# The opening of a hybrid attention block in another order

## The chip, the cores and the metric

The kernel runs on one core of a Trainium2 chip. The metric is the device time of one execution in microseconds (us), lower is better. The core has five engines with a queue of instructions each: PE (matrix multiply; PEld is its loading of weights), DVE (vector), ACT (activations and copies), POOL (general) and SP, which here only issues DMAs. An engine takes its instructions in the order in which the program writes them, and waits where an operand or a buffer is not ready.

## The reference

One layer of a streaming encoder on x of 1024 tokens by 1024 channels, in float32. Only the first part matters here, the two parallel head groups.

```python
h = rmsnorm(x, g_mix_pre[l])
proj = h @ w_in[l]                       # fq, fk, fv, f_logit, cq, ck, cv
f_logit = f_logit + b_fgt[l]
...
def forgetting_attention(q, k, v, f_logit):
    logf = jax.nn.log_sigmoid(f_logit.astype(jnp.float32))
    c = jnp.cumsum(logf, axis=1).transpose(0, 2, 1)
    # logit[t, s] = q_t.k_s / sqrt(Dh) + c[t] - c[s], for s <= t, 8 heads of 64
...
# chunked attention: 8 heads, own chunk of 64 and 8 chunks before, bias by clipped relative position
y = concat(rmsnorm(y_fox), rmsnorm(y_chk))
x = x + rmsnorm(y @ w_out[l], g_mix_post[l])
# then cross-attention into 256 memory tokens, and a squared-ReLU MLP with 4096 hidden channels
```

## The kernel before

Every product is made of three matmuls on high and low halves (`mm3`, lines 172 to 176): ACT copies an operand to its high half, another engine subtracts to get the low half. PE therefore needs both halves of both operands.

**The opening** (lines 1293 to 1480) is written out by hand. x comes in transposed (`load_xt`, tiles `xf`, two token halves of 512) for the products and by rows (`load_row`, `square`) for the norm. `wv_split` makes the halves of the value weights, `plain_split` those of x times the gain `gp`. `value_part` makes the values of a token half and a head group in four PSUM banks (`value_banks`), twelve matmuls for each bank group and channel block `kc`, eight blocks in all. Since the rows' norms come later, `root` turns the squares into factors `rall`, and `values_out` applies them when it empties the banks; for group 0 it also puts the eight forget-gate logits of each token into `fcol`. For q and k, x itself has to be normed: `root` also makes four diagonal pieces, `spread` multiplies them by ones on PE and copies the result to `rt`, `norm` multiplies x by it and `norm_split` makes new halves in the place of the old ones. The order of products is group 0 half 0, group 1 half 0, group 0 half 1, group 1 half 1.

`forget_gates` (lines 377 to 403) transposes `fcol` to eight rows of 1024 tokens, adds the bias `bfgt`, makes the log-sigmoid in steps on DVE and ACT, and scans along the row for `c`. Its last step stores the rows in `cd` (line 401). `bias_rows` loads the relative bias, lays it out and stores it in `rd` (line 229). Both stores are issued by SP where they are written, at the end of the opening.

**The attention phase** is planned at build time. `Flow` keeps a clock of its own: `put` enters a call for an engine (V is DVE, S is ACT, G is POOL, D is SP's DMAs) with the time from which it may run and its assumed cost, `upto` writes the calls in the order that these give, and `run` writes PE's steps from several streams: values, transposes of probabilities, scores, and the fillers, which are the projections of q, k and v (`project_steps`, `filler_steps`). `Tokens` count free buffers, among them six of the shared pool `u4`, and the two PSUM banks `mm` of the projections. `Stock.pump` loads and splits weight blocks in the order q0, k0, q1, k1, q2, ...; the opening itself loads the first three and splits two (`split_now`), and the planner's first step loads the next ones. `Biases.pump` reads `cd` for the biases of the forgetting heads once `seen["gates"]` has passed. `Outputs.pump` starts the first output products when fourteen `u4` buffers are free. The projection of q0 and k0 is made for token half 0 and then for half 1; half 1 of q takes a bank that half 0 of q has left (lines 691 to 698).

Of the kernel before, what the change touches and what calls it, by code (L numbers as in the profile page):

```python
# [135 lines left out]
def build(ctx, tc, nc, out, t):  # L136
# [58 lines left out]
    bfgt = const.tile([8, 1], F32, name="bfgt")  # L195
# [23 lines left out]
    def bias_rows(part):  # L219
# [9 lines left out]
        nc.sync.dma_start(rd, rrow)  # L229
# [147 lines left out]
    def forget_gates():  # L377

        z, e, l, u = [p1.tile([8, S], F32, tag="klo", bufs=4, name=f"f{n}") for n in "zelu"]
        parts = []  # L380
        for g in range(2):
            tr = mm_tile([8, 4, P], f"ftr{g}", "mm")
            for j in range(4):
                nc.tensor.transpose(tr[:, j, :], fcol[:, g * 4 + j, :], ident)
            parts.append(("V", 0.75, lambda g=g, tr=tr: nc.vector.tensor_scalar(
                z[:, g * HT:(g + 1) * HT], tr.rearrange("p a b -> p (a b)"), bfgt, None, op0=ALU.add)))

        parts += [
            ("V", 0.7, lambda: nc.vector.tensor_scalar(l, z, -1.0, None, op0=ALU.mult)),
            ("V", 1.2, lambda: nc.vector.tensor_tensor(l, l, z, op=ALU.min)),  # L390
            ("S", 1.1, lambda: nc.scalar.activation(e, l, AF.Exp)),
            ("V", 0.7, lambda: nc.vector.tensor_scalar(u, e, 1.0, None, op0=ALU.add)),
            ("S", 2.4, lambda: nc.scalar.activation(l, u, AF.Ln)),
            ("V", 1.3, lambda: nc.vector.scalar_tensor_tensor(e, u, 1.0, e, op0=ALU.subtract, op1=ALU.subtract)),
            ("S", 2.4, lambda: nc.scalar.activation(u, l, AF.Exp, scale=-1.0)),
            ("V", 1.2, lambda: nc.vector.tensor_tensor(e, e, u, op=ALU.mult)),
            ("V", 1.2, lambda: nc.vector.tensor_sub(e, e, l)),
            ("V", 1.3, lambda: nc.vector.scalar_tensor_tensor(e, z, 0.0, e, op0=ALU.min, op1=ALU.add)),
            ("V", 0.9, lambda: nc.vector.memset(u, 0.0)),
            ("V", 2.3, lambda: nc.vector.tensor_tensor_scan(l, e, u, 0.0, op0=ALU.add, op1=ALU.add)),  # L400
            ("D", 0.55, lambda: nc.sync.dma_start(cd, l))]

        return [call for _, _, call in parts]
# [54 lines left out]
    def score_steps():  # L458
# [5 lines left out]
        for n, a in heads:  # L464
            kind, pr = ORDER[n]
            h = pr * 2 + a
            for g in groups(n):
                probs[n, a, g] = {}
                for q in (1, 0) if kind == "f" else (0, 1):
# [9 lines left out]
                    for j, (o, w) in enumerate(pieces):  # L479
# [21 lines left out]
                        if not last:  # L501
                            flow.put("V", flow.end, 0.1 + w / 1000, reduce, free["s"].give)
                        else:
# [6 lines left out]
                            rest = [("S", 0.25 + nk / 1090, exp), ("V", 0.17, inv), ("G", 0.25 + nk / 1150, mul)]  # L510
# [10 lines left out]
                            go = lambda at, w=w, reduce=reduce, after=after: flow.put("V", at, 0.1 + w / 1000, reduce, after)  # L521
# [329 lines left out]
    class Outputs:  # L851
# [5 lines left out]
        def pump(self):  # L857
            while self.left:
                th, g = self.left[0]
                if not (there(("od", g)) and ((th, g) == (0, 0) or there("keys")) and free["u4"].ready(14 if (th, g) == (0, 0) else 9)):  # L860
                    break
# [431 lines left out]
    with tc.manual_schedule():  # L1293
# [34 lines left out]
        for i in range(2):  # L1328
            list(load_wv(1, i))
        vs = [[u4(f"vs{g}_{i}", (P, 2, 4, P)) for i in range(4)] for g in range(2)]  # L1330
        for kp in range(2):
            list(load_xt(1, kp))
        for b in range(3):
            load_row(b)
        for kp in range(2, 4):
            list(load_xt(1, kp))

        def wv_split(g, i, eng, cut=False):
# [6 lines left out]
            for c in (slice(0, 1), slice(1, n)) if cut else (slice(0, n),):  # L1345
                nc.scalar.activation(w[0][:, c, :], raw[:, c, :], AF.Copy)
                eng.tensor_sub(w[1][:, c, :], raw[:, c, :], f(w[0][:, c, :]))
            return [(w[0][:, j, :], w[1][:, j, :]) for j in range(n)]
# [17 lines left out]
        def root(th):  # L1366
# [4 lines left out]
            for b in range(4):  # L1371
                nc.gpsimd.tensor_scalar(d[:, b, :], ident, r[:, b:b + 1], 1.0, op0=ALU.mult, op1=ALU.mult)
# [42 lines left out]
        w0 = wv_split(0, 0, nc.vector, True)  # L1415
        for kc in range(3):
# [23 lines left out]
        for kc in range(2):  # L1440
            plain_split(1, kc)
        values_out(0, 0, V)
        for kc in range(2, 4):
            plain_split(1, kc)
        spread(0, d, "s")
        for kc in range(4, 8):
            plain_split(1, kc)
        for kc in range(4):
            norm(0, kc)
# [701 lines left out]
```

## Time and profile before

| | |
|---|---|
| time, median of 3 runs | 1519.47 us (1517.37 to 1520.83) |
| the profiled execution | 1516.47 us, span 1514.7 us |
| mean granted PE clock | 0.993 |
| PE busy | 1468.5 us (97%) |
| DVE busy | 929.5 us (61%) |
| ACT busy | 795.5 us (53%) |
| POOL busy | 390.7 us (26%) |

The profile is of one execution. The span runs from its first instruction to its last; the time holds a little more. A view of one engine's instructions gives start, duration, engine, line, operation, output and input, and in brackets the idle time just before with what ended it. A matmul's end is modelled.

### The profile page before, as it was taken

What the parts mean: (1) busy time and instruction counts of PE and PEld (TensorE: products, weight loads), DVE (VectorE), ACT (ScalarE), POOL (GpSimd) and SP (SyncE); (2) the same over time, 40 slices, a digit from 0 to 9 for tenths busy, and PEclk for the clock granted to TensorE, in tenths of its full rate; (3) what the DMA queues carried; (4) which work ended last, traced back from release to release, by engine and by line L of the source; (5) the groups of instructions that cost most, each with busy time, mean ns of one, the idle gap of its engine ahead of it and who ended that gap; (6) DMA issues with size and microseconds to landing.
All of it is one profiled execution on the core that took longest, in us unless ns stands there. A gap on an engine that the chain in (4) does not pass through costs nothing. (4 is left out here: it accounts for less than half of the span.)

```text
span 1514.7 us, 21395 instructions
## 1 busy us (share of the span) xinstructions
PE 1468.5 (97%) x7564; PEld 1248.1 (82%) x7564; DVE 929.5 (61%) x1585; ACT 795.5 (53%) x1424; POOL 390.7 (26%) x472
## 2 busy tenths in 40 slices
PE   7859999999999999999999999999999999999998
PEld 7748888888888988888888887888888888888886
DVE  3746756654645854795465578665545675746577
ACT  5626766754656864464344455554555543444442
POOL 2324434532332720241021321443333000000021
PEclk9979999999999999999999999999999999999999
DMA  7132233343134577563252256674445695436575
GB/s 265 56 113 57 79 89 83 99 131 85 53 93 118 177 253 287 184 211 116 69 183 61 70 181 215 240 241 152 153 153 181 220 349 209 138 125 204 185 250 195
DMA packets 95227, 239.54 MB, mean 158 GB/s; under 512 B 11768, under 2 KB 20096, under 8 KB 95120
## 3 DMA queue, kind: packets, MB, share of 16 engines
q1 hardware_dynamic: 95120, 238.18, 46.8%
q8 instruction: 59, 0.97, 0.3%
q14 instruction: 48, 0.39, 0.1%
HBM read 170.44 MB, written 59.30 MB: 152 GB/s over the span
## 5 line engine op out<-in xcount | busy, mean ns | idle before, releaser
L571 DVE TENSOR_TENSOR pl<-ptr,ph 128x512 fp32r<-128x512 f32 (+1 forms) x152 | 91.0, 616 | 57.7 <-ACT ph L574 57.4
L1875 ACT ACTIVATE whif<-ra 128x1024 fp32r<-128x1024 f32 x37 | 39.2, 1060 | 123.0 <-PE fy L175 62.6
L1877 DVE TENSOR_TENSOR wlof<-ra,whif 128x1024 fp32r<-128x1024 f32 x37 | 45.3, 1225 | 91.7 <-ACT whif L1875 91.7
L574 ACT ACTIVATE ph<-ptr 128x512 fp32r<-128x512 f32 (+1 forms) x152 | 77.5, 539 | 37.5 <-PE ptr L565 34.2
L1991 POOL TENSOR_SCALAR rf<-sf 128x1 f32<-128x1 f32 x8 | 8.3, 1032 | 326.6 <-ACT jf L1976 326.3
L174 PE MATMUL q<-hT_hi,whiq 128*128 128x512 f32 x128 | 51.8, 405 | 18.7 <-DVE qs L695 18.7
L174 PE MATMUL fx<-vhif,whif 128*128 128x512 f32 x168 | 65.4, 389 | 0.0
L176 PE MATMUL fx<-vhif,wlof 128*128 128x512 f32 x168 | 65.4, 389 | 0.0
L175 PE MATMUL fx<-vlof,whif 128*128 128x512 f32 x168 | 65.4, 389 | 0.0
L605 PE MATMUL pv<-pl,vs 128*128 128x256 f32 (+1 forms) x304 | 64.6, 294 | 0.7 <-DVE pl L571 0.7
L605 PEld LDWEIGHTS pv<-ph,vs 128*128 128x128 f32 x304 | 53.0, 189 | 8.3 <-ACT ph L574 0.5
L1765 POOL TENSOR_TENSOR sc<-wf,wf 128x512 f32<-128x512 f32 x14 | 22.7, 1621 | 142.5 <-DMA wf<-in_w_ff 90.0
L605 PE MATMUL pv<-ph,vs 128*128 128x256 f32 (+1 forms) x304 | 57.4, 270 | 0.1
L174 PE MATMUL k<-hT_hi,whik 128*128 128x512 f32 x128 | 51.8, 405 | 0.0
L174 PE MATMUL mq<-h2T_hi,whimq 128*128 128x512 f32 x128 | 51.6, 403 | 0.0
L175 PE MATMUL q<-hT_lo,whiq 128*128 128x512 f32 x128 | 50.6, 395 | 0.0
L174 PE MATMUL yw<-whiwo,yT_hi 128*128 128x512 f32 x128 | 50.5, 395 | 0.0
L176 PE MATMUL q<-hT_hi,wloq 128*128 128x512 f32 x128 | 50.5, 395 | 0.0
L174 PE MATMUL ym<-whimo,oT_hi 128*128 128x512 f32 x128 | 50.3, 395 | 0.1
L175 PE MATMUL k<-hT_lo,whik 128*128 128x512 f32 x128 | 50.1, 391 | 0.0
L176 PE MATMUL k<-hT_hi,wlok 128*128 128x512 f32 x128 | 50.1, 391 | 0.0
L175 PE MATMUL mq<-h2T_lo,whimq 128*128 128x512 f32 x128 | 50.0, 391 | 0.0
(596 smaller groups left out, 4996.3 us busy)
## 6 DMA issues: line engine op xcount, KB each, us to landing
ra<-gd SPq DMA_DIRECT2D x56, 512.0 KB, 3.7
wg<-in_w_ff SPq DMA_DIRECT2D x56, 512.0 KB, 4.8
wf<-in_w_ff SPq DMA_DIRECT2D x38, 512.0 KB, 3.8
gd<-s SPq DMA_DIRECT2D x48, 256.0 KB, 2.1
wrawmq<-in_w_mq SPq DMA_DIRECT2D x16, 512.0 KB, 3.9
wrawmo<-in_w_mo SPq DMA_DIRECT2D x16, 512.0 KB, 3.7
gd<-u SPq DMA_DIRECT2D x32, 256.0 KB, 2.1
gd<-g SPq DMA_DIRECT2D x25, 256.0 KB, 2.4
```

What stands on the lines that cost most here:

```text
L174: nc.tensor.matmul(ps, lh, rh, start=start, stop=False, skip_group_check=more)
L175: nc.tensor.matmul(ps, lh, rl, start=False, stop=False, skip_group_check=more)
L176: nc.tensor.matmul(ps, ll, rh, start=False, stop=stop, skip_group_check=more)
L571: flow.put("V", at, 0.66, lambda: nc.vector.tensor_sub(pl[:, live, :], tr[:, live, :], f(ph[:, live, :])), done)
L574: flow.put("S", flow.end, 0.58, lambda ph=ph, tr=tr, live=live: nc.scalar.activation(ph[:, live, :], tr[:, live, :], AF.Copy), split)
L605: nc.tensor.matmul(pv[:, q0:q0 + k1 - k0, :], v, x[:, k0:k1, :], start=c == 0 and m == 0, stop=c + 1 == len(steps) and m == 3, skip_group_ ...
L1765: eng.tensor_sub(sc[:, k1], r0[:, k0], r1[:, k0])
L1875: nc.scalar.activation(ah, ra, AF.Copy)
L1877: nc.vector.tensor_sub(al, ra, f(ah))
L1991: nc.gpsimd.tensor_scalar(r, ssf[b][:, 0:1], ssf[b][:, 1:2], EPS, op0=ALU.add, op1=ALU.add)
```

## The change

- The gates are computed on token rows: the bias is laid on all 128 partitions (`bfgt` becomes 128 by 8), eight adds make z of 128 by 64, and every step of the log-sigmoid runs on that shape. Only then does PE transpose (`turn`), ACT copies to eight rows, and `scan` runs as before.
- The store to `cd` and the store to `rd` are entered in the planner's DMA list at its times 7 and 14, and DVE and ACT start there at 7 and 4.
- Of the rows of x, two (3 and 7) get buffers of the pool `u4` and the others use fewer shared ones; the first four are loaded ahead of the second half of the transposed x.
- The first weight column and the first piece of x are split ahead of the rest of that weight block.
- Products, spreads, squares and splits are written in another order; the diagonal pieces go from POOL to DVE.
- In the planner, some assumed costs change, and `Outputs.pump` asks for 12 free buffers for its first part.

```diff
-    bfgt = const.tile([8, 1], F32, name="bfgt")
+    bfgt = const.tile([P, 8], F32, name="bfgt")
...
         nc.vector.tensor_copy(rrow[:, 0:511], rrow[:, 511:512].to_broadcast([8, 511]))
-        nc.sync.dma_start(rd, rrow)
...
+        z, e, l, u = [p1.tile([P, TB, 8], F32, tag="fg", bufs=4, name=f"f{n}") for n in "zelu"]
+        ea, la, ua = [p1.tile([8, S], F32, tag="klo", bufs=4, name=f"f{n}a") for n in "elu"]
+        vec, act = nc.vector, nc.scalar
+        calls = [lambda b=b: vec.tensor_add(z[:, b, :], fcol[:, b, :], bfgt) for b in range(TB)]
+        rows_ = lambda: [calls.pop(0)() for _ in range(TB)]
+        parts = [
+            rows_,
+            lambda: vec.tensor_scalar(l, z, -1.0, None, op0=ALU.mult),
+            lambda: vec.tensor_tensor(l, l, z, op=ALU.min),
+            lambda: act.activation(e, l, AF.Exp),
+            lambda: vec.tensor_scalar(u, e, 1.0, None, op0=ALU.add),
+            lambda: act.activation(l, u, AF.Ln),
+            lambda: vec.scalar_tensor_tensor(e, u, 1.0, e, op0=ALU.subtract, op1=ALU.subtract),
+            lambda: act.activation(u, l, AF.Exp, scale=-1.0),
+            lambda: vec.tensor_tensor(e, e, u, op=ALU.mult),
+            lambda: vec.tensor_sub(e, e, l),
+            lambda: vec.scalar_tensor_tensor(e, z, 0.0, e, op0=ALU.min, op1=ALU.add)]
+
+        def turn(g):
+            tr = mm_tile([8, 4, P], f"ftr{g}", "s")
             for j in range(4):
-                nc.tensor.transpose(tr[:, j, :], fcol[:, g * 4 + j, :], ident)
...
+                nc.tensor.transpose(tr[:, j, :], e[:, g * 4 + j, :], ident)
+            act.activation(ea[:, g * HT:(g + 1) * HT], tr.rearrange("p a b -> p (a b)"), AF.Copy)
+
+        def scan():
+            vec.memset(ua, 0.0)
+            vec.tensor_tensor_scan(la, ea, ua, 0.0, op0=ALU.add, op1=ALU.add)
+
+        return parts, turn, scan, lambda: nc.sync.dma_start(cd, la)
...
-                            flow.put("V", flow.end, 0.1 + w / 1000, reduce, free["s"].give)
+                            flow.put("V", flow.end, 0.36 + w / 1250, reduce, free["s"].give)
...
-                            rest = [("S", 0.25 + nk / 1090, exp), ("V", 0.17, inv), ("G", 0.25 + nk / 1150, mul)]
+                            rest = [("S", 0.42 + nk / 1040, exp), ("V", 0.17, inv), ("G", 0.25 + nk / 1150, mul)]
...
-                    flow.put("V", at, 0.66, lambda: nc.vector.tensor_sub(pl[:, live, :], tr[:, live, :],
+                    flow.put("V", at, 0.56 if dead else 0.7, lambda: nc.vector.tensor_sub(pl[:, live, :], tr[:, live, :],
...
-                flow.put("S", flow.end, 0.58, lambda ph=ph, tr=tr, live=live: nc.scalar.activation(
+                flow.put("S", flow.end, 0.49 if dead else 0.6, lambda ph=ph, tr=tr, live=live: nc.scalar.activation(
...
-  free["u4"].ready(14 if (th, g) == (0, 0) else 9)
+  free["u4"].ready(12 if (th, g) == (0, 0) else 9)
...
         def load_row(b):
-            tag, n = ("sp", 5) if b % 3 == 0 else ("bias", 2)
-            r = p1.tile([P, D], F32, tag=tag, bufs=n, name=f"x_{b}")
+            if b % 4 == 3:
+                r = u4(f"x_{b}", (P, D), F32)
+            else:
+                r = p1.tile([P, D], F32, tag="bias" if b % 4 else "sp", bufs=2 if b % 4 else 5, name=f"x_{b}")
...
+        for b in range(4):
+            load_row(b)
+        for kp in range(4):
+            list(load_xt(1, kp))
         vs = [[u4(f"vs{g}_{i}", (P, 2, 4, P)) for i in range(4)] for g in range(2)]
-        for kp in range(2):
-            list(load_xt(1, kp))
-        for b in range(3):
-            load_row(b)
-        for kp in range(2, 4):
-            list(load_xt(1, kp))
...
-                nc.gpsimd.tensor_scalar(d[:, b, :], ident, r[:, b:b + 1], 1.0, op0=ALU.mult, op1=ALU.mult)
+                nc.vector.tensor_scalar(d[:, b, :], ident, r[:, b:b + 1], 1.0, op0=ALU.mult, op1=ALU.mult)
...
-        w0 = wv_split(0, 0, nc.vector, True)
-        for kc in range(3):
+        w0, rest = wv_split(0, 0, nc.vector, True)
+        plain_split(0, 0)
+        rest()
+        for kc in range(1, 3):
             plain_split(0, kc)
...
         V = value_banks(0, 0)
         value_part(V, 0, w0, range(KC))
         w1 = wv_split(1, 0, nc.gpsimd)
-        for b in range(3):
+        w1 += wv_split(1, 1, nc.gpsimd)
+        for b in range(4):
             square(b)
-        load_row(3)
-        w1 += wv_split(1, 1, nc.gpsimd)
-        square(3)
         for b in range(4, 8):
             load_row(b)
-        nc.sync.dma_start(bfgt, t["b_fgt"])
+        nc.sync.dma_start(bfgt, t["b_fgt"].to_broadcast([P, 8]))
         nc.sync.dma_start(gcol, t["g_heads"])
-        d = root(0)
         stock.load(3)
         W = value_banks(1, 0)
         value_part(W, 0, w1, range(KC))
-        for kc in range(2):
+        d = root(0)
+        values_out(0, 0, V)
+        for kc in range(8):
             plain_split(1, kc)
...
         V = value_banks(0, 1)
-        value_part(V, 1, w0, range(KC))
+        value_part(V, 1, w0, range(4))
         values_out(1, 0, W)
+        spread(0, d, "pv")
+        value_part(V, 1, w0, range(4, 8))
         for b in range(4, 8):
             square(b)
-            norm(0, b)
+        for kc in range(KC):
+            norm(0, kc)
         d = root(1)
         for kc in range(KC):
             norm_split(0, kc)
-        spread(1, d, "pv")
         W = value_banks(1, 1)
-        value_part(W, 1, w1, range(4))
+        value_part(W, 1, w1, range(3))
+        gparts, turn, scan, gate_store = forget_gates()
         values_out(0, 1, V)
-        gates = forget_gates()
-        value_part(W, 1, w1, range(4, 8))
-        for _ in range(2):
-            gates.pop(0)()
+        spread(1, d, "s")
+        value_part(W, 1, w1, range(3, 6))
+        for call in gparts[:4]:
+            call()
         stock.split_now(2)
-        for kc in range(KC):
+        for kc in range(4):
             norm(1, kc)
-            if kc > 1 and gates:
-                gates.pop(0)()
+        for call in gparts[4:6]:
+            call()
+        for kc in range(4, KC):
+            norm(1, kc)
+        for call in gparts[6:]:
+            call()
+        for g in range(2):
+            turn(g)
+        value_part(W, 1, w1, range(6, 8))
+        for kc in range(4):
+            norm_split(1, kc)
+        scan()
+        for kc in range(4, KC):
+            norm_split(1, kc)
         values_out(1, 1, W)
-        for kc in range(KC):
-            norm_split(1, kc)
-            if gates:
-                gates.pop(0)()
-        for call in gates:
-            call()
         bias_rows(0)
         bias_rows(1)
-        seen["gates"] = 9.0
+        seen["gates"] = 11.0
+        flow.put("D", 7.0, 0.55, gate_store, None, -1)
+        flow.put("D", 14.0, 0.55, lambda: nc.sync.dma_start(rd, rows[0]))
+        flow.free.update(V=7.0, S=4.0)
         km, vmh, vml = attention_phase()
```

More of the change, by code (lines that the diff above doesn't have):

```diff
@@ L377, in forget_gates @@
     def forget_gates():
[L379 to L382, printed above, removed]
-            for j in range(4):
-                nc.tensor.transpose(tr[:, j, :], fcol[:, g * 4 + j, :], ident)
-            parts.append(("V", 0.75, lambda g=g, tr=tr: nc.vector.tensor_scalar(
-                z[:, g * HT:(g + 1) * HT], tr.rearrange("p a b -> p (a b)"), bfgt, None, op0=ALU.add)))
@@ L388, in forget_gates @@
[L388 to L401, printed above, removed]
@@ L519, in after @@
                                 flow.chain(at, rest, mark(key), 0)
-                            go = lambda at, w=w, reduce=reduce, after=after: flow.put("V", at, 0.1 + w / 1000, reduce, after)
+                            go = lambda at, w=w, reduce=reduce, after=after: flow.put("V", at, 0.36 + w / 1250, reduce, after)
                             if kind == "f":
@@ L859, in pump @@
                 th, g = self.left[0]
-                if not (there(("od", g)) and ((th, g) == (0, 0) or there("keys")) and free["u4"].ready(14 if (th, g) == (0, 0) else 9)):
+                if not (there(("od", g)) and ((th, g) == (0, 0) or there("keys")) and free["u4"].ready(12 if (th, g) == (0, 0) else 9)):
                     break
@@ L1344, in wv_split, with part @@
             n = raw.shape[1]
-            for c in (slice(0, 1), slice(1, n)) if cut else (slice(0, n),):
+            def part(c):
                 nc.scalar.activation(w[0][:, c, :], raw[:, c, :], AF.Copy)
                 eng.tensor_sub(w[1][:, c, :], raw[:, c, :], f(w[0][:, c, :]))
-            return [(w[0][:, j, :], w[1][:, j, :]) for j in range(n)]
+            part(slice(0, 1 if cut else n))
+            both = [(w[0][:, j, :], w[1][:, j, :]) for j in range(n)]
+            return (both, lambda: part(slice(1, n))) if cut else both
         hT = [Act(f"hT{h}") for h in range(2)]
```

11 lines of the change are left out of this document (1 added, 10 removed).

## The prediction

> **What bounds the kernel now.** The page's first line was read first, then the waits of the matmul engine (PE) in the first 130 us (engine, operation and line, what it waited for, us in total, times, longest), then the busy time of each engine in stretches of the rest.
>
> ```profile
> span 1514.7 us, 21395 instructions
> ...
> PE q L174 <- DVE qs L695: 18.7, 1, 18.7
> PE v L174 <- ACT hT_hi L1355: 8.1, 1, 8.1
> PE rt L1377 <- POOL diag L1372: 5.1, 1, 5.1
> ...
> 115.00:500.00 385.00, 382.86 (x2311) 334.96 (x2310) 230.05 (x658) 241.32 (x521) 153.08 (x233) 1.00 0.33 95
> 500.00:550.00 50.00, 47.71 (x342) 43.99 (x341) 38.92 (x104) 38.01 (x83) 28.02 (x27) 1.00 0.55 171
> ```
>
> In the stretch rows the first pair of numbers is the length and PE's busy time. From 115 to 500 us PE lacks 2.1 us of 385, from 500 to 550 it lacks 2.3 of 50. The attention phase is bound by PE. The opening is not: three waits cost 31.9 us there, 18.7 of them in one piece. Whatever the opening loses, the end loses, because PE has no slack behind it to make it up. So the question is what each of the three waits becomes.
>
> The 18.7 us wait was followed back through the timelines of DVE (vector), ACT (scalar), SP (which issues the DMAs) and DVE again, and the waits of SP's queue (columns: start, duration, engine, line, operation).
>
> ```profile
> 95.09 1.39 DVE L695 SCALAR_TENSOR_TENSOR qs<-q,qs 64x512 fp32r<-64x512 f32 x2 [6.29 <-ACT qs L694]
> ...
> 79.13 1.04 ACT L312 ACTIVATE whiq<-wrawq 128x1024 fp32r<-128x1024 f32 x1
> 92.92 1.06 ACT L312 ACTIVATE whik<-wrawk 128x1024 fp32r<-128x1024 f32 x1 [12.75 <-DMA wrawk<-in_w_qk]
> 93.88 1.18 ACT L694 ACTIVATE qs<-q 64x512 fp32r<-64x512 f32 x2
> ...
> 85.92 0.30 SPq L401 DMA_DIRECT2D cd<-fl  x1
> 89.28 0.35 SPq L299 DMA_DIRECT2D wrawk<-in_w_qk  x1
> ...
> SPq L401 <- DVE fl L400: 42.3, 1, 42.3
> ...
> 83.63 2.27 DVE L400 TENSOR_TENSOR_SCAN fl<-fe,fu 8x1024 f32<-8x1024 f32 x1
> ```
>
> Read upwards. PE needs a PSUM bank that the first q product still holds. ACT must empty it (93.88), but stands in its own queue behind the high half of the second k block (92.92), which waits for its load. That load is issued only at 89.28, because SP has stood 42.3 us at the store of the forget gates (L401), and that store waits for the scan that ends the gate chain at 85.9. Nothing in q or k needs the gates so early. It is the order of one DMA queue.
>
> **The change part by part.** The store of the gates and that of the bias row (`rd`) leave the written order and go into the planner's DMA list, at its times 7 and 14, behind the loads that the planner's first step issues. SP then meets the load of the second k block ahead of the store. The wait of 42.3 us has no successor: the load's price is 92.92 less 89.28, 3.6 us, counted below. What now decides is when PE reaches the second half of q, and that has to be walked. These rows carry the durations.
>
> ```profile
> 4.18 0.42 ACT L1346 ACTIVATE whiv<-wv 128x264 fp32r<-128x264 f32 x1 [2.18 <-DMA wv<-in_w_v]
> 7.38 2.09 ACT L1355 ACTIVATE hT_hi<-xf,gp 128x512 fp32r<-128x512 f32 x3
> ...
> 8.14 0.59 PE L174 MATMUL v<-whiv,hT_hi 128*128 128x264 f32 x1 [8.14 <-ACT hT_hi L1355]
> 34.31 1.02 PE L1377 MATMUL rt<-diag,ones 128*128 128x512 f32 x2
> 46.67 0.28 PE L176 MATMUL v<-whiv,hT_lo 128*128 128x264 f32 x1
> 53.10 1.20 PE L174 MATMUL v<-whiv,hT_hi 128*128 128x256 f32 x1
> 60.23 1.03 PE L384 MATMUL ftr<-ident,fcol 128*8 128x128 f32 x8
> 66.85 0.40 PE L174 MATMUL q<-hT_hi,whiq 128*128 128x512 f32 x1
> 77.53 0.39 PE L176 MATMUL k<-hT_hi,wlok 128*128 128x512 f32 x1
> 96.63 0.77 PE L174 MATMUL q<-hT_hi,whiq 128*128 128x512 f32 x1 [18.71 <-DVE qs L695]
> 103.58 0.39 PE L174 MATMUL k<-hT_hi,whik 128*128 128x512 f32 x1
> ...
> 20.31 20.95 SPq L1318 DMA_DIRECT2D x<-in_x  x5
> ...
> L1362 ACT ACTIVATE junk<-x 128x1024 bf16<-128x1024 f32 x8 | 8.4, 1060 | 9.0 <-DMA x<-in_x 8.7
> 54.13 0.60 ACT L1379 ACTIVATE rt<-rt 128x512 f32<-128x512 f32 x1 [4.16 <-PE rt L1377]
> 46.39 1.56 POOL L1369 TENSOR_TENSOR rall<-rall,mhalf 128x4 f32<-128x4 f32 x1
> 46.36 5.09 DVE L1390 TENSOR_TENSOR hT_lo<-xf,hT_hi 128x512 fp32r<-128x512 f32 x8
> 72.06 1.64 DVE L1412 SCALAR_TENSOR_TENSOR vs<-v,rall,vs 128x256 fp32r<-128x256 f32 x4
> ```
>
> *Start.* The first column of weights and the first piece of x are split ahead of the rest. The weight's high half ends at 4.18 + 0.42 = 4.6, the high half of x takes 0.7 (a third of 2.09), so PE starts at 5.3, not 8.14. Bounds: 2.8 us gained if x and the gains have landed by 4.6, nothing if not. Their loads were issued before that of the weights that landed at 4.18, so 2.8 is taken.
>
> *To the first spread.* From 8.14 to 34.31 PE does the value products of token half 0, in 26.2 us, with no wait. From 5.3 that ends at 31.5. The rows of x in own buffers end SP's 20.95 us among the x loads, so squares, root and the emptying of the first banks come earlier; they are not on the path, since 11.6 us of products stand between. The `bfgt` load, now to 128 partitions, and three weight loads stand behind them on SP and come earlier too, at no cost. The spread moves behind half of the next product: that product took 34.31 + 1.0 to 46.95, so a half is 5.8, the spread starts at 37.3 and its copy ends at 39.0.
>
> *To the second spread.* ACT now squares the other four rows only after that copy: 4 x 1.06 and a read, 43.4. The root takes 1.56 and about 0.4 of hops (an estimate): 45.4. The four diagonal pieces go from POOL to DVE; bounds are nothing and 0.27 each (a quarter-width row below), taken at the upper end: 46.4. Then DVE has eight low halves (5.1) and three of four value lows (1.2) before a bank of the pair that the spread needs is free: 52.7. PE has meanwhile ended the product (44.2) and three eighths of the next (48.6), so it waits 4.1 us. The 5.1 us wait is kept, but 4.4 us of products are now ahead of it.
>
> *To the gates.* Before, four eighths took 53.10 to 60.23 at a slow pace; three take 5.7, so PE is through at 59.4 and then stands at the transposes of the gates, which now come from the finished rows. Is the gate chain ready? It needs these.
>
> ```profile
> 39.26 2.73 DVE L1384 SCALAR_TENSOR_TENSOR xf<-xf,gp,rt 128x512 f32<-128x512 f32 x4
> 45.72 4.25 ACT L1389 ACTIVATE hT_hi<-xf 128x512 fp32r<-128x512 f32 x8
> 71.18 1.51 ACT L1409 ACTIVATE vs<-v,rall 128x256 fp32r<-128x256 f32 x4
> 60.35 5.05 POOL L321 TENSOR_TENSOR wlok<-wrawk,whik 128x512 fp32r<-128x512 f32 x2
> ...
> L226 DVE TENSOR_SCALAR rrow<-rsrc 8x256 f32<-8x256 f32 x1 | 0.3, 274 | 0.0
> L390 DVE TENSOR_TENSOR fl<-fl,fz 8x1024 f32<-8x1024 f32 x1 | 1.2, 1206 | 0.0
> L399 DVE MEMSET fu<- 8x1024 f32 x1 | 0.9, 912 | 0.2 <-issue 0.2
> L393 ACT ACT_TABLE_LOAD x1 | 1.3, 1283 | 0.0
> L1411 ACT ACTIVATE fcol<-v,rall 128x8 f32<-128x8 f32 x8 | 2.3, 291 | 0.0
> ```
>
> The chain's vector steps shrink from 1024 elements in a partition (1.2 us) to 64, and eight adds of 8 elements come in. None is in the trace. Above they are bounded by 1.2, below by next to nothing; 0.27, the row at 256 elements, is the nearest and is taken, and 0.3 for ACT's (its row at 8 elements). Two table loads of 1.28 stay. The copy after the second spread ends at 55.3 (as 54.13 + 0.60 lies 1.6 behind 53.10). Adds and two small steps: 55.8. Exponential, two weight highs of 1.04: ACT at 58.2. DVE's four norms (2.73) and one small step: 58.8. Table load and logarithm: 59.8. Four norms and one step: 61.8. The second load is hidden, the exponential ends at 62.1, three steps at 63.2. So PE waits 3.8 us here, a wait that before does not have: its fcol transposes ran between products.
>
> *To q.* Transposes 1.0, the last two eighths 2.9: q starts at 67.1, against 66.85. POOL's low halves of k took 5.05 and end by about 65. The first halves of q and k take 10.9 (66.85 to 77.8), so PE asks for the bank at 78.0. ACT: two gate copies of 0.6 (the row of that width) to 64.8, four highs of 0.53, four more once the last product has read the old ones (69.2), value highs 70.7, q1 and k1 highs 72.8, q's own 1.18: 74.0. DVE, from 65.4: four lows, memset and scan (0.9 + 2.3), four lows, value lows, three small steps, q's low half 1.39: 77.5. The load of the k block is issued after the bias row's, which needs a buffer that the second low half frees, near 66, and lands at 70, ahead of ACT's 71.7. So the bank is free 0.5 us before PE asks. The 18.7 us wait is gone; next to be late is DVE.
>
> *Sum.* PE takes up the second half of q at 78.0 instead of 96.6: 18.6 us. Without the long pause its eight steps run at full pace, 5.5 us (half of 10.9) instead of 6.95 (96.63 to 103.58): 1.5 more. The new 3.8 us pause may slow the clock for itself: nothing, or 7.1 less 4 x 1.46, 1.3 us, as after the 5.1 us pause; 0.6 is taken. Together 19.5 us.
>
> [...] The shortest pause here that was followed by slow matmuls is the 5.1 us one, so this trace cannot choose.
>
> *The planner's numbers.* Costs of the score reductions, exponentials and splits, the buffers asked for by the first outputs (12 instead of 14) and the start times of the engines alter only the order in which the attention phase is written. No row prices an order. The best it can do is to take away PE's idle time to 550 us, 2.1 + 2.3 = 4.4 us. For the worst, the 500 to 550 stretch is the nearest: if 115 to 500 lost at its rate, 4.6%, it would cost 385 x 4.6% less 2.1, 15.6 us. Zero is taken, because the longer stretch is the nearer row.
>
> The profiled execution took 1516.47 us, 1.8 beyond its span, and the median of the runs is 1519.47, 3.0 above it. 1516.5 - 19.5 + 3.0 = 1500.0 us.
>
> **The rivals.** *The wait moves to the bank.* DVE has 0.5 us to spare and the k load 1.7. If the bias row gets the buffer that the last low half frees (73.6), the k load lands at 77.5, ACT splits it to 78.6, empties q at 79.8, DVE at 81.2: 3.2 us of waiting and up to 1.5 of slow clock, 1504.7 us. Small vector steps at 0.4 instead of 0.27 (18 of them, 2.3 us) come to much the same. For it: the tight margin. Against: a quarter of the elements of the row used.
>
> *The order of attention gets worse.* One mechanism: the first outputs start at 12 free buffers and take nine, and three are left for the projections, which need two or three each and are PE's filler. Without filler PE follows DVE and ACT, as from 500 to 550. To end slower than before, 115 to 500 must lose 6.5% (19.5 + 3 + 2.1 of 385): 1522.5 us and more, say 1525. Against: even the thinnest stretch shown loses 4.6%. Milder, it gives 1505 to 1515.
>
> *The planner gains.* The 4.4 us go and the gate steps cost half: 1500 - 4.4 - 2 = 1493.6 us.
>
> *The change does not reach the queue:* the stores might still be written ahead of the loads, and only the start's 2.8 us be won, 1516.7 us. Against: the first loads are issued when the planner's list is first asked, and its time 7 comes later.
>
> **How the numbers follow.** The forecast, within 4 us: 0.58. The wait at the bank, 1504 to 1508: 0.18. The planner gains: 0.08. The order milder but worse, 1505 to 1515: 0.07. Slower: 0.06. No effect: 0.03. A measurement of this kernel can tell 0.2%, 3 us. The range 1492 to 1509 takes in the first three and part of the fourth and leaves out about 0.15. Faster is 0.58 + 0.18 + 0.08 + 0.07 = 0.91, the same 0.03, slower 0.06.
>
> **What would show it.** Right: PE's list of waits has no q behind DVE above 2 us, keeps a spread of 3 to 6 us and has a new one of 2 to 6 at the gates' transposes; the first matmul is near 5.3; the k block's load comes before the gates' store on SP; the second half of q starts near 78. Wrong: a wait of over 5 us at q, or PE below 98% from 115 to 500 us.

## The result and the profile after

The changed kernel takes 1496.29 us (median of 4 runs, 1495.08 to 1498.95); the kernel before took 1519.36 us beside it. The ratio is 0.9851, 95% interval 0.9833 to 0.987. The forecast was 1500.0 us. The profiled execution took 1498.95 us, span 1497.2; that of before took 1516.47, span 1514.7.

The waits of PE in the first 115 us come first again (engine, operation and line, what it waited for, us in total, times, longest).

```profile
PE ftr L399 <- DVE fe L394: 7.3, 1, 7.3
PE v L174 <- ACT hT_hi L1362: 5.4, 1, 5.4
PE rt L1384 <- DVE vs L1419: 3.8, 1, 3.8
PE q L174 <- DVE qs L698: 0.4, 1, 0.4
```

The wait of 18.7 us at q is 0.4. The one at the spread is 3.8 where 4.1 was forecast. The new one at the gates' transposes is 7.3 where 3.8 was forecast. The timelines of PE and SP give the places.

```profile
5.42 0.59 PE L174 MATMUL v<-whiv,hT_hi 128*128 128x264 f32 x1 [5.42 <-ACT hT_hi L1362]
69.46 1.87 PE L399 MATMUL ftr<-ident,fe 128*8 128x128 f32 x8 [7.34 <-DVE fe L394]
74.87 0.40 PE L174 MATMUL q<-hT_hi,whiq 128*128 128x512 f32 x1
86.29 0.47 PE L174 MATMUL q<-hT_hi,whiq 128*128 128x512 f32 x1 [0.35 <-DVE qs L698]
...
61.38 0.35 SPq L298 DMA_DIRECT2D wrawk<-in_w_qk  x1
...
78.40 0.30 SPq L406 DMA_DIRECT2D cd<-fla  x1
```

SP issues the load of the k block 17 us ahead of the gates' store, as forecast; it still waits 13.7 us at that store, but the load no longer stands behind it. But q's second half starts at 86.29, not 78.0. So the opening gave less than the 19.5 us of the forecast, and something else must have given the rest. It is found by the first score, the first product of the next stage (mk) and the first output product (yw), in the groups of PE by tile (the two times in each line are the first and the last start), of before and then of after.

```profile
L492 PE MATMUL sf0g<-kd,qs x12: 281/388/501, 115.1 to 130.9; 128*128 128x512 f32 x5, 128*128 128x256 f32 x4, 128*128 128x384 f32 x3
L174 PE MATMUL mk<-mT_hi,whimk x64: 277/283/367, 489.9 to 535.1; 128*128 128x256 f32 x64
L174 PE MATMUL yw<-whiwo,yT_hi x128: 389/389/486, 535.4 to 655.1; 128*128 128x512 f32 x128
...
L495 PE MATMUL sf0g<-kd,qs x12: 278/389/447, 103.4 to 118.9; 128*128 128x512 f32 x5, 128*128 128x256 f32 x4, 128*128 128x384 f32 x3
L174 PE MATMUL mk<-mT_hi,whimk x64: 277/283/386, 474.3 to 516.5; 128*128 128x256 f32 x64
L174 PE MATMUL yw<-whiwo,yT_hi x128: 389/389/500, 517.4 to 636.9; 128*128 128x512 f32 x128
```

To the first score 11.7 us are gained (115.1 to 103.4). From there to mk it takes 370.9 us instead of 374.8, 3.9 gained; from mk to yw 43.1 instead of 45.5, 2.4 gained; behind that 0.5 is lost. The sum is the 17.5 us between the spans. The medians show 23.1, because the profiled execution of before lies 2.9 us under its median and that of after 2.7 over. The 3.9 and 2.4 us behind the first score, 6.3 together, are where the forecast had put zero.

### The profile page after: what moved, and what is told of

The parts are those of the page before. It is cut to its first block, busy times and chain, and to the rows that moved or that the text cites. A ratio compares the mean times of both kernels' runs of the same rounds, so it can differ in the third digit from the quotient of the medians.

```text
span 1497.2 us, 21427 instructions
## 1 busy us (share of the span) xinstructions
PE 1468.1 (98%) x7564; PEld 1250.3 (84%) x7564; DVE 926.4 (62%) x1599; ACT 794.6 (53%) x1426; POOL 374.6 (25%) x464
## 5 line engine op out<-in xcount | busy, mean ns | idle before, releaser
L1889 DVE TENSOR_TENSOR wlof<-ra,whif 128x1024 fp32r<-128x1024 f32 x37 | 45.3, 1225 | 91.3 <-ACT whif L1887 91.2
L174 PE MATMUL mq<-h2T_hi,whimq 128*128 128x512 f32 x128 | 51.6, 403 | 0.0
```

The source lines that it names most:

```text
L174: nc.tensor.matmul(ps, lh, rh, start=start, stop=False, skip_group_check=more)
L1889: nc.vector.tensor_sub(al, ra, f(ah))
```

## The experiments

**One part alone, on the kernel before: the stores.** Only the two stores go into the planner's list.

```diff
-        nc.sync.dma_start(rd, rrow)
...
+        gate_store = gates.pop()
...
+        flow.put("D", 7.0, 0.55, gate_store, None, -1)
+        flow.put("D", 14.0, 0.55, lambda: nc.sync.dma_start(rd, rows[0]))
```

> The kernel before with one part of the change: the stores of the gates and of the bias row go into the planner's DMA list at 7 and 14, nothing else. Theory (the wait at q has a second holder behind the first): the k block's load is no longer behind the scan, ACT empties q by about 82.3, but DVE is still in its gate chain and row steps until 88.8 and makes q's low half until 90.2; so the second half of q starts near 90.2 instead of 96.6, the wait at q falls from 18.7 to about 12.3, and the time by about 6.4 us, to 1513. Rival (the store alone held q): the second half of q follows the first half of k at 78, the time falls by 18.7 + 1.5, to about 1499.

Measured: 1512.94 us, 0.9964 of before (0.9951 to 0.9977). The waits and DVE's timeline:

```profile
PE q L174 <- DVE qs L694: 13.4, 1, 13.4
...
89.48 1.34 DVE L226 TENSOR_SCALAR rrow<-rsrc 8x256 f32<-8x256 f32 x1
...
90.86 1.37 DVE L228 COPY rrow<-rrow 8x511 f32<-8x511 f32 x1
92.24 1.39 DVE L694 SCALAR_TENSOR_TENSOR qs<-q,qs 64x512 fp32r<-64x512 f32 x2
```

With the DMA queue free the wait falls by 5.3 us, not by 18.7, and the ratio says 5.5. What holds q's bank now is DVE's own list: wide gate steps, low halves and the bias row, all written ahead of `qs`. In the change the gates on token rows and the new order take the rest away; the two were not tried apart.

**The planner's numbers alone, on the kernel before.** The costs and the 12 of the change, nothing else.

> The kernel before with only the planner's numbers of the change: costs of score reductions, exponentials and splits, and 12 buffers instead of 14; the opening as before. Theory (the numbers make a better order of the attention phase): the first score stays at 115 us, the first output product (yw, 535.4 before) comes 6 us earlier, and the time falls by 4 to 7 us, to about 1513. Rival (the attention phase gained because the opening left its loads and buffers ahead): yw within 1 us of 535.4, the time within 1 us of 1519.4.

Measured: 1511.87 us, 0.9957 (0.9942 to 0.9971). The first score starts no earlier (115.8), yw starts at 530.2 instead of 535.4. These numbers are worth about as much as the stores, 6.5 us by the ratio.

**The changed kernel with the numbers put back.** Old costs, 14 buffers.

> The changed kernel with the planner's numbers of before: old costs and 14 buffers; the opening, the stores in the list and the start times of the engines as in the change. Theory (the numbers make a better order): the first score stays at 103.4, the first output product (517.4 in the changed kernel) comes 5 to 7 us later, and the time rises by 4 to 7 us against the changed kernel, to about 1502. Rival (the gain in the attention phase comes from the opening): within 1 us of the changed kernel, about 1496.

**The changed kernel with one number put back.** 14 buffers, new costs.

```diff
-  free["u4"].ready(12 if (th, g) == (0, 0) else 9)
+  free["u4"].ready(14 if (th, g) == (0, 0) else 9)
```

> The changed kernel with one number put back: 14 buffers counted free in place of 12; the planner's new costs stay. Theory (the costs carry the 3.6 us gained between the first score and the first mask product of the last stage, the 12 carries the 2.4 us gained behind it): first score to first mk stays at 371 us, mk to yw goes back from 43.2 to about 45.6, and the time is 2 to 3 us over the changed kernel's: about 1499. Rival (the 12 carries all of it, since it sets how early the loads of the output weights are let in): first score to first mk goes back to 374.5 and the time is 6 to 9 us over: about 1503.5.

Measured: 1505.53 us, 0.9913 (0.9898 to 0.9928), with all numbers back; 1499.7 us, 0.9877 (0.9863 to 0.989), with the 14 alone. The stretch rows from the first score to mk and from mk to yw (length, PE's busy time, weight loads' busy time) of before, of the old numbers, of the 14 alone, and of after:

```profile
115.10:489.90 374.80, 372.66 (x2227) 324.87 (x2227) 224.57 (x651) 234.07 (x510) 145.49 (x228) 1.00 0.31 88
489.90:535.40 45.50, 44.02 (x351) 42.45 (x350) 37.77 (x101) 37.48 (x80) 30.15 (x27) 1.00 0.56 169
...
102.90:477.40 374.50, 372.35 (x2226) 324.81 (x2225) 224.42 (x651) 234.01 (x510) 145.41 (x228) 1.00 0.31 88
477.40:523.00 45.60, 44.12 (x351) 42.52 (x350) 37.76 (x101) 37.51 (x80) 30.16 (x27) 1.00 0.55 167
...
100.90:471.30 370.40, 369.25 (x2227) 325.05 (x2226) 224.36 (x651) 235.27 (x510) 144.80 (x228) 1.00 0.31 87
471.30:517.60 46.30, 44.80 (x351) 42.71 (x350) 36.74 (x101) 36.40 (x79) 28.77 (x27) 1.00 0.56 173
...
103.40:474.30 370.90, 370.46 (x2235) 326.16 (x2234) 230.51 (x659) 239.67 (x518) 151.55 (x233) 1.00 0.32 93
474.30:517.40 43.10, 42.89 (x348) 42.04 (x347) 32.13 (x94) 33.82 (x73) 19.07 (x22) 1.00 0.51 149
```

The lengths separate cleanly. The costs own the first stretch: about 374.6 us with the old ones, about 370.6 with the new. The 12 owns the second: about 45.5 to 46.3 with 14, 43.1 with 12. The numbers alone on the kernel before, with its old opening, give 371.3 and 43.1, so it is not the opening that shortens these stretches. By the ratios the costs are worth 0.0036 of before, 5.5 us, and the 12 another 0.0015 to 0.0026, 2.3 to 3.9 us (the changed kernel was run twice, 0.9851 and, below, 0.9862). The changed kernel with all numbers back, 0.9913, also gives the price of everything else in the change: 13.2 us.

How the 12 does it stands in the groups of SP by tile: the first load for the output products (first and last start), of the 14 alone and of after.

```profile
L911 SPq DMA_DIRECT2D oin<-od_0h x8: 320/402/464, 470.8 to 536.3; - x8
...
L911 SPq DMA_DIRECT2D oin<-od_0h x8: 376/415/430, 349.6 to 532.6; - x8
```

With 12, the preparation of the first outputs begins 121 us earlier. It then lies under the scores and not in the stretch from mk to yw, where POOL's busy time falls from 28.77 to 19.07 us and DVE's from 36.74 to 32.13.

How the costs do it stands in the waits of the weight loads (PEld), from the first score to 490 us in before, to mk in the kernel with the 14 alone.

```profile
PEld sf0g L492 <- DVE mnf0g L496: 2.2, 5, 0.9
PEld sc2g L492 <- DVE mnc2g L496: 1.4, 3, 0.9
PEld sc4g L492 <- DVE mnc4g L496: 1.4, 3, 0.9
PEld sc0g L492 <- DVE mnc0g L496: 1.4, 3, 0.9
...
PEld sf0g L495 <- DVE mnf0g L499: 1.2, 4, 0.6
PEld sc0g L495 <- DVE mnc0g L499: 0.2, 1, 0.2
```

The planner used to think a score reduction cheaper than it is (0.61 us for 512 columns, where the trace has 0.69 to 0.75 and a read of 0.08) and wrote the next score too early behind it. Such waits on reductions come to 9.5 us in before, smaller rows included, and to about 2 us with the new costs. In the kernel with all numbers put back the same rows stand, 9.6 us in all, so the new opening does not remove them. Beside them the kernel with the 14 alone has 1.7 us of waits on the DMAs of `kd` and `kl`. Not all of the 9.5 us was on the path: the stretch is shorter by 3.9 to 4.4. The costs of exponentials and splits changed with those of the reductions and were not tried apart.

**The splits later.** The wait at the gates' transposes, 7.3 us, was suspected to come from POOL: the low halves of the first q and k blocks run beside DVE's norms. They are put behind the norms.

```diff
-        stock.split_now(2)
         for kc in range(4):
             norm(1, kc)
...
         for call in gparts[6:]:
             call()
+        stock.split_now(2)
```

> The changed kernel with the split of the first q and k weight blocks moved behind the last step of the gate chain, so that POOL's low halves no longer run beside DVE's norms. [...] Rival (the norms are slow because of PE's or ACT's accesses, or the gate steps themselves are long): the norms stay slow, the wait stays at 7 or more, and since the q block's low half now comes later, the time is the same or up to 4 us longer.

Measured: 1496.13 us, 0.9851 (0.9835 to 0.9868), no change. DVE's and POOL's timelines of after, then DVE's with the splits later, then PE's there:

```profile
57.10 4.80 DVE L1391 SCALAR_TENSOR_TENSOR xf<-xf,gp,rt 128x512 f32<-128x512 f32 x4 [1.30 <-ACT rt L1386]
61.82 1.25 DVE L388 TENSOR_SCALAR fu<-fe 128x64 f32<-128x64 f32 x1
62.99 3.78 DVE L1391 SCALAR_TENSOR_TENSOR xf<-xf,gp,rt 128x512 f32<-128x512 f32 x4
58.23 3.12 POOL L320 TENSOR_TENSOR wloq<-wrawq,whiq 128x512 fp32r<-128x512 f32 x2 [10.83 <-ACT whiq L311]
61.31 2.93 POOL L320 TENSOR_TENSOR wlok<-wrawk,whik 128x512 fp32r<-128x512 f32 x2
...
58.62 2.74 DVE L1391 SCALAR_TENSOR_TENSOR xf<-xf,gp,rt 128x512 f32<-128x512 f32 x4 [1.31 <-ACT rt L1386]
61.38 2.73 DVE L1391 SCALAR_TENSOR_TENSOR xf<-xf,gp,rt 128x512 f32<-128x512 f32 x4
69.27 4.69 DVE L1397 TENSOR_TENSOR hT_lo<-xf,hT_hi 128x512 fp32r<-128x512 f32 x4 [2.63 <-ACT hT_hi L1396]
...
85.25 0.77 PE L174 MATMUL q<-hT_hi,whiq 128*128 128x512 f32 x1 [2.16 <-DVE qs L698]
85.81 0.63 PE L175 MATMUL q<-hT_lo,whiq 128*128 128x512 f32 x1
...
88.89 0.40 PE L174 MATMUL q<-hT_hi,whiq 128*128 128x512 f32 x1
```

The suspicion holds: eight norms take 5.5 us without POOL (0.68 each, where 0.74 was expected) and 8.6 beside it, and the small step at L388, 0.18 with the splits later, takes 1.25. The wait at the transposes falls from 7.3 to 3.1 us, where 3.6 was expected. But the end does not move, where 3 to 4 us less, about 1492.5, were expected. The splits now meet DVE's low halves instead (four take 4.69 us, and 2.50 in the changed kernel), `qs` is late, and 2.2 us of the wait come back at q. The pause also halves the pace of the next seven matmuls (0.43 us from start to start against 0.23), 1.4 us more. From the second spread to the end of q's second half 36.5 us are left of 37.5, and 1 us is less than these runs can tell.

**The splits later, and DVE's other steps too.** The same, with the gate scan, the second row of biases and their stores put behind q's low half.

```diff
-        scan()
...
-        bias_rows(1)
-        seen["gates"] = 11.0
-        flow.put("D", 7.0, 0.55, gate_store, None, -1)
-        flow.put("D", 14.0, 0.55, lambda: nc.sync.dma_start(rd, rows[0]))
+        flow.chain(8.6, [("V", 3.2, scan), ("D", 0.55, gate_store)], mark("gates"), 1)
+        flow.chain(13.0, [("V", 0.8, lambda: bias_rows(1)), ("D", 0.55, lambda: nc.sync.dma_start(rd, rows[0]))])
```

> The changed kernel with two edits: the low halves of the first query and key weights are split behind the norms of the last pieces (as in the run that split them late), and now VectorE's gate scan with its store and the second row of biases with its store are put off until behind q's low half. Theory (VectorE's list of steps ahead of qs sets the end of the opening: each step taken out of it shortens the wait at q's bank): the wait of q on qs, 2.2 us in the run that split late, falls below 0.4 us, the seven matmuls at half pace behind it (1.4 us) go, and the time is 3 to 4 us under the changed kernel's: about 1492.5. Rival (the tensor engine is held by something else right behind, ScalarE's split of the key weights or the k projection): the wait comes back at the next product and the time stays within 1 us of 1496.

Measured: 1491.23 us, 0.9823 (0.9809 to 0.9836). The wait at q is gone from PE's list, and the second half of q runs at full pace from its start:

```profile
PE ftr L399 <- DVE fe L394: 3.7, 1, 3.7
...
80.96 0.39 PE L174 MATMUL q<-hT_hi,whiq 128*128 128x512 f32 x1
```

**All late steps elsewhere.** The splits go the other way, ahead of the first spread, where DVE stands idle; the pieces of the last product are all issued ahead of the transposes; scan and bias row stay behind q's low half. One row of x gets another buffer, the third weight block is loaded a little later, and the planner's start times of DVE and ACT change (6 and 5.2 instead of 7 and 4).

```diff
+        stock.split_now(2)
         spread(0, d, "pv")
...
-        value_part(W, 1, w1, range(3, 6))
+        value_part(W, 1, w1, range(3, 8))
...
-        for g in range(2):
-            turn(g)
-        value_part(W, 1, w1, range(6, 8))
         for kc in range(4):
             norm_split(1, kc)
-        scan()
+        for g in range(2):
+            turn(g)
```

> The changed kernel with all that its trace shows late put elsewhere: the low halves of the first query and key weights split early, before the second spread of values; all of that spread's pieces issued to the tensor engine ahead of the gates' transposes; gate scan and second bias row with their stores behind q's low half. Theory (the opening still holds 3.8 + 7.3 us of waits that come from the order of VectorE's and GpSimd's steps alone): the transposes wait 1 us or less, the second half of q starts near 77.4 instead of 86.3, the first score near 95, and the time is 7 to 9 us under the changed kernel's: about 1488. Rival (early splits on GpSimd stretch VectorE's steps wherever they are put): the waits move to the second spread or to the k projection, and the gain is under 3 us.

Measured: 1488.07 us, 0.9803 (0.979 to 0.9817). It beats both kernels. Its waits, POOL's split and DVE's norms in the new place, and the second half of q:

```profile
PE rt L1386 <- DVE vs L1421: 3.8, 1, 3.8
PE ftr L399 <- DVE fe L394: 0.3, 1, 0.3
...
33.27 2.55 POOL L320 TENSOR_TENSOR wloq<-wrawq,whiq 128x512 fp32r<-128x512 f32 x2 [10.29 <-ACT whiq L311]
38.37 5.39 DVE L1393 SCALAR_TENSOR_TENSOR xf<-xf,gp,rt 128x512 f32<-128x512 f32 x8 [5.55 <-ACT rt L1388]
...
74.33 0.39 PE L174 MATMUL q<-hT_hi,whiq 128*128 128x512 f32 x1
```

POOL ends before DVE's norms begin, eight of which take 5.39 us. The transposes wait 0.3 us. The first score comes at 91.3 us, against 100.7 in the profile of the changed kernel that got its full pace at the same time (below). Of the opening's waits behind the start only the spread's 3.8 us is left: DVE has to empty the bank that PE has just filled.

**The start undone, and the kernel once more.** The whole first weight block is split before the first piece of x again.

```diff
-        plain_split(0, 0)
         rest()
+        plain_split(0, 0)
```

> The changed kernel with the early split of the first piece undone: the tensor engine's first product waits for the whole first split again, all else as changed. Theory (the first products run at the slow clock and then meet the next piece, so an early start is mostly given back by 34 us): first product 2.5 us later, the second spread's start 0.7 us later, time +0.5 to +1 us: about 1497. Rival (my forecast's term: the start moves everything behind it): +2.5 to +2.8 us, about 1499.

Measured: 1499.35 us, 0.9877 (0.9863 to 0.989), first product at 8.82 and first score at 104.6. That is the rival's time. The expectation of 0.7 us came from one trace, so the changed kernel was run again.

> The changed kernel once more, beside the next two on the same chip. In the profiles so far the tensor engine gets its full clock anywhere between 9.5 and 16.7 us, with the same opening in five of them, and the first spread of the second half of x follows at 36.7 to 40.9. Theory (the moment of the clock is chance, and the changed kernel's profiled run had a late one): the times again scatter over 3 to 4 us about 1496.3, and the kernel whose early first split was undone, at 0.9877 of before, stays slower than this one by 0.2 to 0.3%, the 2.8 us that my forecast gave the start. Rival (the start gives only the 0.7 us that the two first traces show): this one comes out at 0.987 of before, with the other.

Measured: 1497.78 us, 0.9862 (0.9841 to 0.9883). The start is worth 0.0015 of before, 2.3 us, by this ratio, and 0.0026, 3.9 us, by the first one. Each of these differences is uncertain by about 0.0025 itself, so the start's worth is not settled: the forecast's 2.8 lies between the two values and 0.7 below both, but neither is excluded. The four times range over 6.4 us, more than expected. The two profiles of the same kernel show why one trace misled. The stretch from 10 to 15 us, of the first profile and of this one:

```profile
10.00:15.00 5.00, 5.00 (x24) 5.00 (x24) 4.59 (x8) 5.00 (x8) 0.00 (x0) 1.00 1.03 408
...
10.00:15.00 5.00, 5.00 (x43) 5.00 (x42) 4.63 (x8) 5.00 (x8) 0.00 (x0) 1.00 1.03 393
```

The same busy share, 24 matmuls in one and 43 in the other. PE goes from 0.22 us a matmul to 0.12 at 15.1 us in the first and at 9.6 in the second, and the first score follows at 103.4 and at 100.7.

**Products ahead of the inputs.** Eight products of constants fill PE's first wait, in the changed kernel and in the one with all late steps elsewhere.

```diff
+        warm = mm_tile([P, P], "warm", "tr")
+        for i in range(8):
+            nc.tensor.matmul(warm, ones, ones, start=True, stop=True)
         w0, rest = wv_split(0, 0, nc.vector, True)
```

> The changed kernel with eight products of the constant ones (128x128, float32) put on the tensor engine ahead of its first real product, into a bank that is free then; their result is not read. They fill the wait of 5.3 us for the first inputs. Theory (the full clock comes some time after the engine has been kept busy): the full clock comes by 9 us in place of 9.5 to 16.7, the first spread by 37, and the time is 1 to 2.5 us under the changed kernel's: about 1494.5. Rival (the clock comes at moments of its own, whatever ran before, or the inputs pace the first products anyway): no earlier spread, same time.

> The kernel with all late steps put elsewhere (1488.07 us, 0.9803 of before) with the same eight products ahead. Theory: its profiled run already had the full clock at 9.5 us, so its best runs can't gain, its median up to 2 us: about 1486.5. Rival: no change, 1488.

Measured: 1497.33 us, 0.9857 (0.984 to 0.9874), and 1488.13 us, 0.9795 (0.978 to 0.9809). Neither differs from its kernel without them, so the expected gains of 1 to 2.5 us did not come. In the first, PE had the faster pace at 6.37 us, ran out of inputs, and lost it again. In the second the first real products ran at the slow pace, mostly 0.22 us from start to start, and the full one, 0.12, came at 13.5 us.

The rows of the first:

```profile
1.10 3.50 PE L1424 MATMUL warm<-ones 128*128 128x128 f32 x16 [1.10 <-DVE ones L194]
6.37 0.29 PE L174 MATMUL v<-whiv,hT_hi 128*128 128x264 f32 x1
9.82 0.39 PE L174 MATMUL v<-whiv,hT_hi 128*128 128x264 f32 x1 [2.20 <-ACT hT_hi L1362]
...
10.00:15.00 5.00, 4.73 (x25) 4.53 (x26) 4.62 (x7) 4.73 (x8) 0.00 (x0) 0.66 1.03 415
```

## Why the prediction was right in the sum, and where its steps were wrong

The sum came within 3.7 us of the median by two errors of opposite sign, and that they nearly cancel is luck. The opening was forecast at 19.5 us; it gave 11.7 to the first score in the first profile, 14.4 in the second, and 13.2 by the ratio with the old numbers. The planner was forecast at zero and gave 6.3 or more. The direction and the mechanism of the opening held. Of the signs named ahead, the wait at q, the spread, the start and the order on SP came out; the wait at the transposes (7.3 us, where 2 to 6 was named) and the start of q's second half (86.3, where 78 was named) did not.

- *The store queue.* Right that the 42.3 us wait of SP had no successor on SP and that DVE is next to be late. The stores alone gave 5.5 us, since DVE's list stood right behind.
- *Start.* Right: 5.42 against 5.3. What it is worth at the end was measured as 2.3 and as 3.9 us, against 2.8, and is not settled closer.
- *To the first and second spread.* Right within what the moment of PE's full pace moves. The first spread was forecast at 37.3 and came at 39.4 and 36.7 in the two profiles of the kernel, the second at 52.7 and came at 54.4 and 51.6; the wait of 4.1 us is 3.8. The 0.4 us of hops in the root was an estimate that no row shows; from the last square's read (its end at 45.25) to the first diagonal piece (47.44) the first profile has 2.2 us, where 1.96 was counted.
- *To the gates.* This is the step that failed. The term was DVE's eight norms at 2.73 for four. The row was measured where POOL stood still, and the change put POOL's splits beside them. Measured 4.80 and 3.78, which with the step at L388 makes up the difference between 7.9 us forecast for the chain from the copy of the spread to the transposes and the 12.2 measured (57.1 to 69.3). With the splits later it takes 8.0. In before POOL and the norms met too, but there the norms kept their time and POOL was the one that was stretched (5.05 for k's two halves against 2.55 for q's), and I took that row as POOL's price rather than as a warning. The second table load was not hidden, but stands with its 1.28 us behind a wait for DVE's step at L390 (the first, at 59.12, ran ahead of its activation); the small steps, 0.2 to 0.23 instead of 0.27 and eight adds in 0.69, gave much of that back.

The rows show that the two get in each other's way, in both directions: in the changed kernel four norms take 4.80 and 3.78 us beside POOL's splits, and 2.74 and 2.73 with the splits later; in before POOL's low halves of k take 5.05 us beside DVE's steps, against 2.55 for those of q while DVE stood still. Smaller steps of DVE were stretched as well: L388 takes 1.25 us against 0.18, and the bias row's L226 1.05 us in the changed kernel, where POOL splits from 78.57 to 85.91 us, against 0.28 with DVE's steps later, where POOL is done by then. What decides which of the two is stretched is not shown.

- *To q.* Failed by what came before it, and by a second term: behind the 7.3 us pause the transposes and the first nine of the 24 matmuls of PE's last two eighths were slow, so that together they took 69.46 to 74.87, 5.4 us against 3.9. The second half of q came 8.3 us later than forecast: 1.7 were there at the second spread, 4.6 came up to the transposes, 1.5 from the slow pace, 0.5 at the bank. In the second profile, with the early full pace, it came at 83.6, 5.6 us late; the gates' 4.6 are the same there. DVE's margin of 0.5 us at the bank came out at -0.4. The slow pace behind a pause had been a term of 0.6 us; it is the 1.5, a little above the upper bound of 1.3.
- *The planner's numbers.* Taken as zero, with a gain of at most 4.4 us. They gave 6.3 by the stage lengths, and by the ratios (0.9913 with the old ones) 7.8 to 9.4. The bound failed, not only the choice. It counted PE's idle time, but PE's busy time holds stalls as well: from the first score to mk about the same matmuls took 372.66 us of busy time before and 370.46 after, while idle time fell from 2.1 to 0.4. The waits of the weight loads show these stalls, 9.5 us of them, and were not read.
- *The rivals.* The wait did not move to the bank in the change (0.4 us), but did so at once when the splits were moved (2.2 us). The planner's gain was a rival at 0.08 and is what happened, beside an opening that fell short. There is no sign of the order of attention getting worse: PE is busy for 384.55 of the 385 us from 115 to 500. (The 6.5% that this rival needs comes to 6.4% by its own terms.)

## What to carry to other kernels

A price taken from a trace holds for the neighbours that it had there (four norms took 2.73 us alone and 4.80 beside POOL): before an instruction of DVE is costed at its old duration, look at what POOL will do beside it in the new order. Bound what a better order can give by the waits of the weight loads as well as by idle PE, because a stalled matmul counts as busy (372.66 us of busy time against 370.46 from the first score to mk). And when a wait is taken out, look at the whole list of steps that the next engine has written ahead of the same point; moving only the splits moved the wait, moving all the late steps gave 8.2 us more by the medians.

## What the runs showed of the hardware

The moment at which PE reaches its full pace (matmuls of the value products 0.12 us from start to start, where those before it have mostly 0.22) differs between executions of one program: the two profiles of the changed kernel have it at 15.1 and 9.6 us, and the profiles of the other kernels with the same start at 9.5 to 16.9. Between the two profiles the first score moves by 2.7 us, about as much as the start that the change gains. Chance is not the whole of it: where the thirteenth matmul follows the twelfth without a gap, the full pace comes at 9.5 and 9.6 us, and where it starts 1.3 to 1.9 us later, at 13.4 to 16.9. But behind nearly the same 0.55 and 0.57 us it comes at 9.8 in one profile and at 15.1 in another, so late inputs alone do not decide it. The column of the granted clock reads 1.00 in both stretches; the count of matmuls shows the pace. Between the two executions of one program 5.5 us lie, and what decides the moment is not shown.

PE also slowed behind short pauses: seven matmuls at half pace behind 2.16 us of waiting at q (granted clock 0.66 from 85.25 to 90 us), and half pace from 11.1 to 14.4 us behind 2.20 us with the constant products (granted clock 0.66 from 10 to 15 us). The fall need not follow at once: with the splits later, PE still runs at full pace behind the 3.1 us at the transposes, and the half pace begins at 68.0 us, 1.2 us behind the end of that wait. Whether what ran ahead of the pause matters was not tried.
